# One streaming-encoder step: the input norm's gain row comes by DMA, and the first two x tiles are scaled before they are split

## The chip, the cores and the metric

The kernel runs on one core of a Trainium2 chip. The metric is device time in microseconds (us) of one execution, as a median of several. One execution was also taken by the hardware profiler, and every line of a profile below comes from such an execution.

The core has five engines that run their own instruction streams and wait for each other by semaphores: PE (matrix products and transposes), DVE (vector work), ACT (activations and copies), POOL (vector work as well) and SP, which here only issues transfers. PSUM is the memory that PE writes its products to; SBUF is the large on-chip memory.

## The reference

One layer on 2048 prompt frames and 64 frames of a running stream, width 1024, all in 32-bit floats:

```python
def rms_norm(x, g):
    xf = x.astype(jnp.float32)
    y = xf * lax.rsqrt(jnp.mean(xf * xf, axis=-1, keepdims=True) + EPS)
    return (y * g.astype(jnp.float32)).astype(x.dtype)

def mixer_layer(x, ln_g, w_in, lb, norm_g, w_out, attn_fn, s0):
    B, T, _ = x.shape
    aq, ak, av, ag, hq, hf, hi, hg = jnp.split(rms_norm(x, ln_g) @ w_in, SPLITS, axis=-1)
    heads = lambda a: a.reshape(B, T, H_A, DH_A)
    k = heads(ak)
    v = heads(av)
    o_a = attn_fn(heads(aq), k, v).reshape(B, T, W_A) * jax.nn.silu(ag)
    o_b, S = hgrn2_branch(hq, hf, hi, hg, lb, norm_g, s0)
    y = x + jnp.concatenate([o_a, o_b], axis=-1) @ w_out
    return y, k, v, S
```

`attn_fn` is a banded attention over 64-frame chunks (8 heads of 64), `hgrn2_branch` a gated linear recurrence whose forget gate is `f = lb + (1-lb) sigmoid(W_f x)` (4 heads of 128), with `lb` a softmax over two rows of `lb_gamma`. The result goes through a last RMSNorm. The change touches only how the first `rms_norm` and the first columns of `w_in` are brought to PE.

## The kernel before, in words

The frames are worked in four blocks of 512 to 576. For each block the normalised x is brought to PE as two parts that PE takes in its faster 32-bit form: `xh`, the rounded value, and `xl`, what rounding left. Each 128 columns of `w_in` (32 such pieces, "weights" below) are split in the same way into a pair `w[:, 0]` and `w[:, 1]`. `project` makes one piece of the projection by 8 products of xh by the first part, 8 of xl by the first part, and 8 of xh by the second part, added up in one PSUM tile `acc`. In the first block, the first two weights are used in two halves of 256 frames (x tiles 0 and 1, then x tiles 2 and 3), all others on 512 frames at once.

Before the first product the following must happen to each x tile of 128 frames (`x_tile`, `x_split`): it lands (SP's transfer), ACT squares and sums it (L368) and makes the reciprocal root (L336, L337), DVE scales it by that and by the gain row `ln_in_g` in two halves of 512 columns (L382), PE transposes four blocks of 128 columns at a time into a PSUM tile named tr, pv or g (L253), ACT rounds it to xh (L408), DVE subtracts to get xl (L412). Tile 3 and weights 2 and 3 land in the rooms `kd` and `v`, which the attention uses later, so the trace calls them so.

DVE's gain row must stand in all 128 partitions. Before, 4 KB of it are loaded into one partition, and two products of a row of ones by it (L1970) spread it over a PSUM tile `s`; DVE reads it there, and ACT copies it to SBUF later (L1948) for the other blocks. While nothing else is ready, PE runs products of the identity (`spinning`, L1959).

POOL rounds the first three weights (L462) and DVE the rest (L465); POOL makes all the second parts in four pieces of 256 columns (L470). Then the pair is stored to DRAM for the later blocks (L479). `forget_bounds` makes `lb` and `1 - lb` (`oml`) with four tiny DVE instructions (L302 to L305), which the first forget gate needs (L1249, L1250, then a running sum, L1256).

The order of the instructions on every engine is set by a planner (`Plan`), run when the program is built: threads of work say when they may go on, by times that it estimates for the engines or by conditions on what was issued, and the first ready thread of the best priority issues its next piece. Nothing is decided on the chip: each engine takes its list in order, and an instruction that waits holds all behind it on that engine. The planner's own clock only sets that order.

Of the kernel before, what the change touches and what calls it, by code (L numbers as in the profile page):

```python
# [17 lines left out]
P = 128  # L18
# [165 lines left out]
def hymba_step(  # L184
# [105 lines left out]
    def forget_bounds():  # L290

        lmx = T(cst, [P, NHB], F32, "lmx")
        le = T(cst, [P, 2, NHB], F32, "le")
        dve.tensor_tensor(lmx, lbg[:, 0], lbg[:, 1], ALU.max)
        for i in range(2):
            dve.tensor_sub(le[:, i], lbg[:, i], lmx)
        t = C.dve(300)
        yield lambda: "r1" in have
        act.activation(le, le, AF.Exp)
        t = C.act(8, t)  # L300
        yield lambda: "s1" in have
        dve.tensor_add(lmx, le[:, 0], le[:, 1])  # L302
        dve.reciprocal(lmx, lmx)
        dve.tensor_mul(lb, le[:, 0], lmx)
        dve.tensor_scalar(oml, lb, -1.0, 1.0, ALU.mult, ALU.add)  # L305
        C.dve(400, t)
        have.add("bounds")
# [43 lines left out]
    def x_tile(sb, half, c, here=None, gain=None):  # L351
# [21 lines left out]
        if not sb:  # L373
            yield lambda: "gain" in have and (not half or x_there.get((0, 0, 1), (0, 0))[0] == 4)
        g = g_in[:rows] if gain is None else gain
# [27 lines left out]
    def x_split(sb, half, c, rows, k0, tag, pt, t):  # L403
# [6 lines left out]
        there(sb, half, k0, 0, t)  # L410
        yield "D", t
# [23 lines left out]
    def weights():  # L435


        for j, (sb, nt) in enumerate(order):
            if sb:
                yield lambda: j - 1 in w_at  # L440
                yield from tk["w"].get()
                w = w_pair()
                sp.dma_start(f32(w), wd[nt])
                t = C.dma(1024)
                w_at[j] = (w, t, t)
                continue
# [9 lines left out]
    def w_split(j, nt, raw, t, tok):  # L456
# [4 lines left out]
        if j < 3:  # L461
# [7 lines left out]
        for k in range(0, KT, 2):  # L469
            pool.tensor_sub(w[:, 1, k : k + 2], raw[:, k : k + 2], f32(w[:, 0, k : k + 2]))  # L470
            t = C.pool(320, t)
            if k == 0:
                w_at[j] = (w, th, t + 2500.0)
            if k < KT - 2:
                yield "P", t - 300.0
# [59 lines left out]
    def project(j, ranges, evac, close=True, ready=None):  # L535
# [5 lines left out]
        for off, bn in ranges:  # L541
# [3 lines left out]
            for i, (wi, x) in enumerate(((0, xh), (0, xl), (1, xh))):  # L545
                if i == 2:
                    yield tl
                for kt in range(KT):
                    if ready and i < 2 and kt % 4 == 0:
                        yield lambda: ready(i, kt)  # L550
# [1357 lines left out]
    def program():  # L1908


        constants()
        kroom = f32(T(pa, [P, 2, WIN + NMAX], F32R, "kd")).rearrange("p a c -> p (a c)")
        vroom = f32(T(pa, [P, 2, 9, 2, 64], F32R, "v")).rearrange("p h t s d -> p (h t s d)")
        act.dma_start(g_in[0:1], ln_in_g.rearrange("(o d) -> o d", o=1))
# [10 lines left out]
        for what, i in (("x", 0), ("x", 1), ("w", 0), ("x", 2), ("w", 1), ("x", 3), ("w", 2), ("w", 3)):  # L1925
            if what == "x":
                sp.dma_start(xr0[i], x_rows(0, i * P, P))
            else:
# [6 lines left out]
        gps = s_ps()  # L1935
        tk["g"].take()
        tk["s_ps"].take()
# [3 lines left out]
        def first_x():  # L1941
            for c in range(4):
                C.spawn(x_tile(0, c // 2, c * P, (xr0[c], landed["x", c]),
                               gps.rearrange("p a c -> p (a c)")), 0)
            yield lambda: x_there.get((0, 1, 1), (0, 0))[0] == 4
            tk["xn"].put(3, C.now)
            yield "A", C.now
            act.copy(g_in, gps.rearrange("p a c -> p (a c)"))  # L1948
            tk["s_ps"].put(1, C.act(1024))
            for a in (f32(ql[64:128, 0]), f32(ql[0:64, 1])):  # L1950
                yield "P", 0.0
                pool.memset(a, 0.0)
                C.pool(300)
# [10 lines left out]
        for _ in range(4):  # L1964
            spinning()
            C.now += 400.0
            yield None

        for a in range(2):
            pe.matmul(gps[:, a], f32(ones)[0:1], g_in[0:1, a * 512 : a * 512 + 512], start=True, stop=True)  # L1970
            C.now += 1000.0
            yield None
        have.add("gain")
        for _ in range(3):
            spinning()
            C.now += 330.0
# [188 lines left out]
```

## Time and profile before

| what | us |
|---|---|
| median of three runs (1252.43 to 1253.24) | 1253.23 |
| the profiled execution, its own time | 1252.94 |
| its span, first to last instruction | 1251.2 |
| PE busy in it | 1237.5 (99%) |
| DVE, ACT, POOL busy | 888.8, 684.5, 412.4 |
| first product of the projection starts | 12.18 |
| PE runs on without a shown gap from | 23.78 |

The span is 1.7 us shorter than the execution's own time. In the rows of the timeline the columns are: start, duration, engine, line, operation, the tile written and the tiles read with their shape, how many alike were merged (the duration is then that of all), and in brackets the idle time before it and what ended it. PE's matmul records overlap, since its products are pipelined; the time from one to the next is what counts. Where the same row is said to have a pitch, that is this time.

### The profile page before, as it was taken

Reading aid. Unit: us, or ns where it says so; the run is one execution under the profiler, and the core shown is the slowest. Engines: PE = TensorE matmul, PEld = TensorE weight load, DVE = VectorE, ACT = ScalarE, POOL = GpSimd, SP = SyncE. Lnnn points to the kernel's source line nnn. Section 1 sums busy time; section 2 is a strip of 40 time slices with the busy share of each in tenths; the row PEclk is TensorE's granted clock in tenths of the full one; section 3 lists DMA queues with packets and bytes.
Section 4 is the critical chain, followed back from the end, with each engine's and each line's share of the span. In section 5 each row is a group of like instructions: output and inputs, shape, how many; then the busy total and the mean of one; then the engine's idle time right before and its main releaser. Section 6 shows DMA issues by size and latency. Waiting matters only on the chain. (4 is left out here: it accounts for less than half of the span.)

```text
span 1251.2 us, 21385 instructions
## 1 busy us (share of the span) xinstructions
PE 1237.5 (99%) x7526; PEld 1089.1 (87%) x7526; DVE 888.8 (71%) x1889; ACT 684.5 (55%) x1533; POOL 412.4 (33%) x702
## 2 busy tenths in 40 slices
PE   8999999999999999999999999999999999999997
PEld 7888888999999999998888888988888888888786
DVE  6688879766767677686576667775857476867775
ACT  6354546655556556674465556664656445643443
POOL 6766565111110110201233242133241103474543
PEclk9999999999999999999999999999999999999999
DMA  8987979666554476654777778677666665888431
GB/s 331 335 289 242 333 268 350 207 181 223 166 186 155 146 250 192 202 165 164 274 257 249 279 261 281 224 252 255 217 245 208 215 215 207 330 272 248 144 119 67
DMA packets 137956, 287.94 MB, mean 230 GB/s; under 512 B 35257, under 2 KB 79289, under 8 KB 120186
## 3 DMA queue, kind: packets, MB, share of 16 engines
q1 hardware_dynamic: 137560, 286.58, 67.7%
q8 instruction: 59, 0.97, 0.3%
q14 instruction: 47, 0.39, 0.1%
q10 hardware_dynamic: 290, 0.01, 0.0%
HBM read 195.31 MB, written 92.27 MB: 230 GB/s over the span
## 5 line engine op out<-in xcount | busy, mean ns | idle before, releaser
L249 PE MATMUL acc<-xh,w 128*128 128x512 f32 (+2 forms) x2752 | 568.7, 345 | 0.6 <-ACT xh L408 0.6
L249 PEld LDWEIGHTS acc<-xh,w 128*128 128x128 f32 x2752 | 437.7, 189 | 49.7 <-ACT xh L408 1.0
L249 PE MATMUL acc<-xl,w 128*128 128x512 f32 (+2 forms) x1376 | 292.8, 345 | 1.6 <-DVE xl L412 1.6
L249 PEld LDWEIGHTS acc<-xl,w 128*128 128x128 f32 x1376 | 220.8, 189 | 26.6 <-DVE xl L412 2.0
L946 ACT CAST ph<-tr 128x512 fp32r<-128x512 f32 (+3 forms) x176 | 87.9, 507 | 86.9 <-PE pv L249 48.9
L934 ACT ACTIVATE pr<-pr,nm 128x640 f32<-128x640 f32 (+4 forms) x132 | 100.6, 762 | 57.1 <-DVE nm L917 56.5
L470 POOL TENSOR_TENSOR w<-wraw,w 128x256 fp32r<-128x256 f32 x120 | 103.0, 886 | 55.1 <-DVE w L465 48.2
L917 DVE CUSTOM_DVE_ANT_0 pr<-s,bias 128x640 f32<-128x640 f32 (+4 forms) x128 | 94.4, 737 | 37.0 <-PE s L249 36.4
L949 DVE TENSOR_TENSOR ph<-tr,ph 128x512 fp32r<-128x512 f32 (+3 forms) x176 | 101.2, 589 | 25.9 <-ACT ph L946 25.1
L249 PE MATMUL pv<-ph,v 128*128 128x256 f32 (+2 forms) x344 | 97.7, 370 | 0.0
L253 PE MATMUL tr<-ident,pr 128*128 128x128 f32 x580 | 88.4, 272 | 0.9 <-DVE ph L949 0.5
L506 POOL TENSOR_TENSOR xn<-wraw,xn 128x256 fp32r<-128x256 f32 x48 | 39.5, 824 | 141.9 <-ACT xn L503 136.1
L988 DVE TENSOR_TENSOR mixa<-mixa,pv 64x256 f32<-64x256 f32 (+1 forms) x144 | 56.9, 395 | 35.5 <-ACT mixa L984 32.1
L1090 POOL TENSOR_TENSOR mixa<-mixa,sga 128x256 f32<-128x256 f32 (+1 forms) x36 | 28.5, 793 | 162.4 <-DVE mixa L988 150.5
L938 DVE TENSOR_SCALAR pr<-pr,sm 128x640 f32<-128x640 f32 (+4 forms) x132 | 76.3, 578 | 4.7
L253 PEld LDWEIGHTS tr<-ident,pr 128*128 128x128 f32 x580 | 69.8, 140 | 10.6 <-PE acc L249 0.8
L1527 POOL TENSOR_TENSOR k<-ob 128x512 f32<-128x512 f32 (+2 forms) x20 | 17.9, 893 | 179.9 <-ACT ob L1518 139.8
L570 ACT ACTIVATE sig<-acc 128x512 f32<-128x512 f32 (+2 forms) x64 | 32.1, 501 | 62.7 <-PE acc L249 59.9
L249 PEld LDWEIGHTS pv<-ph,v 128*128 128x128 f32 (+1 forms) x344 | 58.3, 189 | 7.0
L984 ACT COPY mixa<-pv 64x256 f32<-64x256 f32 (+1 forms) x72 | 25.2, 351 | 58.6 <-PE pv L249 54.3
L249 PE MATMUL s<-kd,q 128*128 128x320 f32 (+2 forms) x232 | 55.9, 311 | 0.4 <-DVE nm L917 0.4
L249 PE MATMUL s<-kd,ql 128*128 128x320 f32 (+2 forms) x232 | 55.5, 309 | 0.0
(324 smaller groups left out, 2134.5 us busy)
## 6 DMA issues: line engine op xcount, KB each, us to landing
w<-wd SPq DMA_DIRECT2D x96, 1024.0 KB, 5.5
wd<-w SPq DMA_DIRECT2D x32, 1024.0 KB, 7.6
wraw<-in_w_in_dram SPq DMA_DIRECT2D x30, 512.0 KB, 5.5
wod<-xn SPq DMA_DIRECT2D x28, 512.0 KB, 5.8
xn<-in_x_prompt_dram SPq DMA_DIRECT2D x23, 512.0 KB, 4.7
bias<-biasd SPq DMA_DIRECT2D x24, 320.0 KB, 5.4
carry<-kd SPq DMA_DIRECT2D x12, 512.0 KB, 7.0
carry<-v SPq DMA_DIRECT2D x12, 512.0 KB, 5.8
```

Source lines behind the costliest of these rows:

```text
L249: pe.matmul(out, w, x, **kw)
L253: pe.transpose(out, x, idn)
L470: pool.tensor_sub(w[:, 1, k : k + 2], raw[:, k : k + 2], f32(w[:, 0, k : k + 2]))
L506: pool.tensor_sub(f32r(st[:, c.start + 512 : c.stop + 512]), src[:, c], st[:, c])
L570: act.activation(sig[:, :bn], acc, AF.Exp, scale=-1.0)
L917: dve.tensor_tensor_reduce(s[:, :nk].rearrange("p (a c) -> p a c", a=ns), sps[:, :ns, :kn], d.bias[:, h, bcol : bcol + nk].rearrange("p (a ...
L934: act.activation(s[:, :nk], s[:, :nk], AF.Exp, bias=nm[:, 0:1], scale=-1.0, accum_out=sm)
L938: dve.tensor_scalar(s[:, :nk], s[:, :nk], sm, None, ALU.mult)
L946: act.copy(ph[:krows, 0, :wid], pt[:krows, :wid])
L949: dve.tensor_sub(ph[:krows, 1, :wid], pt[:krows, :wid], f32(ph[:krows, 0, :wid]))
L988: dve.tensor_add(mix[hs, :qn], mix[hs, :qn], pv[hs, i, :qn])
L1090: pool.tensor_mul(mix[:, :n], mix[:, :n], d.sg[:, g0 : g0 + n])
```

## The change

The gain row is loaded into all 128 partitions by one transfer on SP's queue, second in line, behind x tile 0. The two products, the PSUM tile for them, ACT's copy and the 4 KB transfer on ACT's queue go away, and DVE reads the gain in SBUF. x tiles 0 and 1 are scaled before either is split, and 2 and 3 likewise: a split's subtraction now waits (in the planner) until the second tile of its pair was scaled. The four instructions of `forget_bounds` wait for x tile 3's scaling where they waited for tile 1's. POOL rounds four weights and no longer three, and takes the pieces of a split without spacing. The two memsets of `ql` are issued at the start. `project` waits (again in the planner) for each quarter of a weight's second part, no longer for all of it. PE runs 12 products of the identity in place of 4, 2 products of ones and 3 more.

```diff
--- before.py
+++ after.py
@@ -298,7 +298,7 @@
         yield lambda: "r1" in have
         act.activation(le, le, AF.Exp)
         t = C.act(8, t)
-        yield lambda: "s1" in have
+        yield lambda: "s3" in have
         dve.tensor_add(lmx, le[:, 0], le[:, 1])
         dve.reciprocal(lmx, lmx)
         dve.tensor_mul(lb, le[:, 0], lmx)
@@ -348,7 +348,7 @@
     x_there = {}
     x_left = {(-1, 0): True, (-1, 1): True}
 
-    def x_tile(sb, half, c, here=None, gain=None):
+    def x_tile(sb, half, c, here=None):
 
         off, bn = SUPER[sb][3][half]
         rows = min(P, off + bn - c)
@@ -371,8 +371,8 @@
         t = C.act(1700, t)
         have.add(f"r{c // P}")
         if not sb:
-            yield lambda: "gain" in have and (not half or x_there.get((0, 0, 1), (0, 0))[0] == 4)
-        g = g_in[:rows] if gain is None else gain
+            yield lambda: not half or x_there.get((0, 0, 1), (0, 0))[0] == 4
+        g = g_in[:rows]
         cut = (slice(0, 512), slice(512, D)) if not sb else (slice(0, D),)
         ends = []
         for k0 in (0, 4):
@@ -408,6 +408,8 @@
         act.copy(dh, src)
         t = C.act(512, t)
         there(sb, half, k0, 0, t)
+        if not sb:
+            yield lambda: f"s{2 * half + 1}" in have
         yield "D", t
         dve.tensor_sub(dl, src, f32(dh))
         t = C.dve(512, t)
@@ -442,7 +444,7 @@
                 w = w_pair()
                 sp.dma_start(f32(w), wd[nt])
                 t = C.dma(1024)
-                w_at[j] = (w, t, t)
+                w_at[j] = (w, t, [t] * 4)
                 continue
             if j in raws:
                 raw, t, tok = raws.pop(j)
@@ -458,7 +460,7 @@
         yield lambda: j == 0 or j - 1 in w_at
         yield from tk["w"].get()
         w = w_pair()
-        if j < 3:
+        if j < 4:
             pool.tensor_copy(w[:, 0], raw)
             t = C.pool(700, t)
         else:
@@ -470,9 +472,10 @@
             pool.tensor_sub(w[:, 1, k : k + 2], raw[:, k : k + 2], f32(w[:, 0, k : k + 2]))
             t = C.pool(320, t)
             if k == 0:
-                w_at[j] = (w, th, t + 2500.0)
+                w_at[j] = (w, th, [])
+            w_at[j][2].append(t + 400.0)
             if k < KT - 2:
-                yield "P", t - 300.0
+                yield "P", 0.0
         if tok:
             tk[tok].put()
         yield t
@@ -543,9 +546,10 @@
             acc = acc_ps()
             n = 0
             for i, (wi, x) in enumerate(((0, xh), (0, xl), (1, xh))):
-                if i == 2:
-                    yield tl
                 for kt in range(KT):
+                    if i == 2 and kt % 2 == 0:
+                        yield lambda: len(tl) > kt // 2
+                        yield tl[kt // 2]
                     if ready and i < 2 and kt % 4 == 0:
                         yield lambda: ready(i, kt)
                     mm(acc[:, :bn], w[:, wi, kt, :], x[:, kt, off : off + bn], bn,
@@ -1909,9 +1913,10 @@
 
 
         constants()
+        for a in (f32(ql[64:128, 0]), f32(ql[0:64, 1])):
+            pool.memset(a, 0.0)
         kroom = f32(T(pa, [P, 2, WIN + NMAX], F32R, "kd")).rearrange("p a c -> p (a c)")
         vroom = f32(T(pa, [P, 2, 9, 2, 64], F32R, "v")).rearrange("p h t s d -> p (h t s d)")
-        act.dma_start(g_in[0:1], ln_in_g.rearrange("(o d) -> o d", o=1))
         act.dma_start(lbg, lb_gamma)
         act.dma_start(g_norm, hg_norm_g)
         xr0 = [T(px, [P, D], F32, "xn", bufs=XNB) for _ in range(3)] + [kroom[:, :D]]
@@ -1922,9 +1927,11 @@
                 tk[tag].take()
         landed = {}
         C.now = 900.0
-        for what, i in (("x", 0), ("x", 1), ("w", 0), ("x", 2), ("w", 1), ("x", 3), ("w", 2), ("w", 3)):
+        for what, i in (("x", 0), ("g", 0), ("x", 1), ("w", 0), ("x", 2), ("w", 1), ("x", 3), ("w", 2), ("w", 3)):
             if what == "x":
                 sp.dma_start(xr0[i], x_rows(0, i * P, P))
+            elif what == "g":
+                sp.dma_start(g_in, ln_in_g.rearrange("(o d) -> o d", o=1).broadcast_to([P, D]))
             else:
                 sp.dma_start(wr0[i], w_in[order[i][1]].rearrange("p (k n) -> p k n", k=KT))
             landed[what, i] = C.dma(640) - 1800.0
@@ -1932,25 +1939,15 @@
         for i in range(4):
             raws[i] = (wr0[i], landed["w", i], "raw" if i < 2 else None)
         spin = psum("g")
-        gps = s_ps()
         tk["g"].take()
-        tk["s_ps"].take()
         C.now = 1400.0
         C._on("P", 4000.0, 0.0)
 
         def first_x():
             for c in range(4):
-                C.spawn(x_tile(0, c // 2, c * P, (xr0[c], landed["x", c]),
-                               gps.rearrange("p a c -> p (a c)")), 0)
+                C.spawn(x_tile(0, c // 2, c * P, (xr0[c], landed["x", c])), 0)
             yield lambda: x_there.get((0, 1, 1), (0, 0))[0] == 4
             tk["xn"].put(3, C.now)
-            yield "A", C.now
-            act.copy(g_in, gps.rearrange("p a c -> p (a c)"))
-            tk["s_ps"].put(1, C.act(1024))
-            for a in (f32(ql[64:128, 0]), f32(ql[0:64, 1])):
-                yield "P", 0.0
-                pool.memset(a, 0.0)
-                C.pool(300)
             yield lambda: 3 in w_at
             tk["kv0"].put()
             tk["kv1"].put()
@@ -1961,19 +1958,9 @@
         C.spawn(first_x(), 0)
         C.spawn(forget_bounds(), 1)
         C.spawn(weights(), 2)
-        for _ in range(4):
+        for _ in range(12):
             spinning()
-            C.now += 400.0
-            yield None
-
-        for a in range(2):
-            pe.matmul(gps[:, a], f32(ones)[0:1], g_in[0:1, a * 512 : a * 512 + 512], start=True, stop=True)
-            C.now += 1000.0
-            yield None
-        have.add("gain")
-        for _ in range(3):
-            spinning()
-            C.now += 330.0
+            C.now += 440.0
             yield None
         tk["g"].put()
 
```

The planner then puts the instructions in another order. At three places:

DVE, the first two x tiles and the step to the next two, before. x tiles 0 to 3 are xn_171, xn_172, xn_173 and kd_166; lmx, lb and oml belong to the forget gate's bounds; tr, pv and g are PSUM tiles with transposes; s_186 is the gain in PSUM:

```order
L382 SCALAR_TENSOR_TENSOR xn_171<-xn_171,rstd_201,s_186 128x512 x2
L382 SCALAR_TENSOR_TENSOR xn_172<-xn_172,rstd_210,s_186 128x512
L412 TENSOR_TENSOR xl_154<-tr_215,xh_153 128x4x128
L382 SCALAR_TENSOR_TENSOR xn_172<-xn_172,rstd_210,s_186 128x512
L302 TENSOR_TENSOR lmx_188<-le_189 128x4
L303 RECIPROCAL lmx_188<-lmx_188 128x4
L304 TENSOR_TENSOR lb_81<-le_189,lmx_188 128x4
L305 TENSOR_SCALAR oml_82<-lb_81 128x4
L412 TENSOR_TENSOR xl_154<-tr_225,xh_153 128x4x128
L412 TENSOR_TENSOR xl_154<-pv_231,xh_153 128x4x128
L412 TENSOR_TENSOR xl_154<-tr_246,xh_153 128x4x128
L382 SCALAR_TENSOR_TENSOR xn_173<-xn_173,rstd_262,s_186 128x512 x2
```

The same place with the change (x tiles 0 to 3 are xn_172, xn_173, xn_174 and kd_168, and gin_152 is the gain in SBUF):

```order
L382 SCALAR_TENSOR_TENSOR xn_172<-xn_172,rstd_203,gin_152 128x512 x2
L382 SCALAR_TENSOR_TENSOR xn_173<-xn_173,rstd_221,gin_152 128x512 x2
L414 TENSOR_TENSOR xl_154<-tr_212,xh_153 128x4x128
L414 TENSOR_TENSOR xl_154<-tr_225,xh_153 128x4x128
L414 TENSOR_TENSOR xl_154<-pv_235,xh_153 128x4x128
L414 TENSOR_TENSOR xl_154<-g_246,xh_153 128x4x128
L382 SCALAR_TENSOR_TENSOR xn_174<-xn_174,rstd_262,gin_152 128x512 x2
L382 SCALAR_TENSOR_TENSOR kd_168<-kd_168,rstd_285,gin_152 128x512 x2
L414 TENSOR_TENSOR xl_154<-tr_297,xh_153 128x4x128
```

All four halves of tiles 0 and 1 are scaled first, the four subtractions follow without a break, the bounds have gone from here, and then tiles 2 and 3 are scaled together.

DVE, from there to the last subtraction of tiles 2 and 3, before (w_346 is weight 3, sig and gk are the forget gate, gb its running sum, gq another gate):

```order
L382 SCALAR_TENSOR_TENSOR kd_166<-kd_166,rstd_277,s_186 128x512
L412 TENSOR_TENSOR xl_154<-tr_300,xh_153 128x4x128
L382 SCALAR_TENSOR_TENSOR kd_166<-kd_166,rstd_277,s_186 128x512
L1249 TENSOR_SCALAR sig_318<-sig_318,oml_82,lb_81 128x256
L1250 TENSOR_SCALAR gk_310<-sig_318 128x256
L465 CAST w_346<-v_167 128x1024
L412 TENSOR_TENSOR xl_154<-tr_325,xh_153 128x4x128
L412 TENSOR_TENSOR xl_154<-pv_333,xh_153 128x4x128
L1256 SCALAR_TENSOR_TENSOR gb_311<-reset_78,sig_318 128x256
L412 TENSOR_TENSOR xl_154<-tr_355,xh_153 128x4x128
L575 TENSOR_TENSOR gq_309<-acc_312,sig_382 128x256
```

And with the change:

```order
L414 TENSOR_TENSOR xl_154<-tr_297,xh_153 128x4x128
L302 TENSOR_TENSOR lmx_189<-le_190 128x4
L303 RECIPROCAL lmx_189<-lmx_189 128x4
L304 TENSOR_TENSOR lb_81<-le_190,lmx_189 128x4
L305 TENSOR_SCALAR oml_82<-lb_81 128x4
L414 TENSOR_TENSOR xl_154<-tr_316,xh_153 128x4x128
L1253 TENSOR_SCALAR sig_339<-sig_339,oml_82,lb_81 128x256
L1254 TENSOR_SCALAR gk_337<-sig_339 128x256
L414 TENSOR_TENSOR xl_154<-pv_324,xh_153 128x4x128
L414 TENSOR_TENSOR xl_154<-g_355,xh_153 128x4x128
L579 TENSOR_TENSOR gq_336<-acc_307,sig_381 128x256
L1260 SCALAR_TENSOR_TENSOR gb_338<-reset_78,sig_339 128x256
```

The bounds now stand between the subtractions of tile 2's two halves, behind all the scaling; the rounding of weight 3 has left DVE; the running sum has moved behind the last subtraction.

POOL, the first weights, before (w_221, w_265, w_296 and w_346 are the pairs of weights 0 to 3):

```order
L462 CAST w_221<-wraw_174 128x1024
L470 TENSOR_TENSOR w_221<-wraw_174,w_221 128x256 x3
L462 CAST w_265<-wraw_175 128x1024
L470 TENSOR_TENSOR w_221<-wraw_174,w_221 128x256
L470 TENSOR_TENSOR w_265<-wraw_175,w_265 128x256
L462 CAST w_296<-kd_166 128x1024
L470 TENSOR_TENSOR w_265<-wraw_175,w_265 128x256 x2
L470 TENSOR_TENSOR w_296<-kd_166,w_296 128x256
L470 TENSOR_TENSOR w_265<-wraw_175,w_265 128x256
L470 TENSOR_TENSOR w_296<-kd_166,w_296 128x256
L470 TENSOR_TENSOR w_346<-v_167,w_346 128x256
L470 TENSOR_TENSOR w_296<-kd_166,w_296 128x256
```

And with the change, where these are w_233, w_275, w_361 and w_391, and w_464 and w_473 are weights 4 and 5:

```order
L1917 MEMSET ql_155 64x704 x2
L464 CAST w_233<-wraw_175 128x1024
L472 TENSOR_TENSOR w_233<-wraw_175,w_233 128x256 x4
L464 CAST w_275<-wraw_176 128x1024
L472 TENSOR_TENSOR w_275<-wraw_176,w_275 128x256 x4
L464 CAST w_361<-kd_168 128x1024
L472 TENSOR_TENSOR w_361<-kd_168,w_361 128x256
L464 CAST w_391<-v_169 128x1024
L472 TENSOR_TENSOR w_361<-kd_168,w_361 128x256 x3
L472 TENSOR_TENSOR w_391<-v_169,w_391 128x256 x4
L472 TENSOR_TENSOR w_464<-wraw_266,w_464 128x256 x4
L472 TENSOR_TENSOR w_473<-wraw_344,w_473 128x256 x4
```

Weights 0 and 1 are now done one after the other, weight 3 is rounded here, and the memsets of ql stand ahead of all. On SP the list is x0, gain, x1, w0, x2, w1, x3, w2, w3 where it was the same without the gain. From a little over half of the program on, all five engines have the same instructions in the same order as before.

## The prediction, made before the changed kernel was run

> **What bounds the kernel now.** I read the page first, then PE's list of waits, then the timelines of PE, DVE, POOL and ACT over the first 35 us, the only part that the change is written for.
>
> ```profile
> span 1251.2 us, 21385 instructions
> PE 1237.5 (99%) x7526; PEld 1089.1 (87%) x7526; DVE 888.8 (71%) x1889; ACT 684.5 (55%) x1533; POOL 412.4 (33%) x702
> ```
>
> PE has work in 99% of the span, so only what PE loses can be won: 13.7 us in all. Its longest wait:
>
> ```profile
> PE acc L249 <- DVE xl L412: 1.6, 2, 1.4
> ```
>
> It lies at the start. On PE:
>
> ```profile
> 7.14 1.65 PE L1959 MATMUL g<-ident 128*128 128x128 f32 x6
> 8.58 1.91 PE L253 MATMUL tr<-ident,xn 128*128 128x128 f32 x8
> ...
> 12.18 0.72 PE L249 MATMUL acc<-xh,w 128*128 128x256 f32 x4
> ...
> 15.23 1.34 PE L249 MATMUL acc<-xl,w 128*128 128x256 f32 x8 [1.39 <-DVE xl L412]
> ...
> 17.13 0.60 PE L253 MATMUL tr<-ident,xn 128*128 128x128 f32 x4
> ...
> 20.94 2.16 PE L249 MATMUL acc<-xh,w 128*128 128x256 f32 x16
> 22.94 0.64 PE L249 MATMUL acc<-xl,w 128*128 128x256 f32 x4
> 23.78 0.74 PE L249 MATMUL acc<-xl,w 128*128 128x256 f32 x4 [0.20 <-DVE xl L412]
> ...
> 31.84 3.79 PE L249 MATMUL acc<-xh,w 128*128 128x512 f32 x16
> ```
>
> Products begin at 12.18, stop until the xl of tiles 0 and 1 is there at 15.23, and run on from then but for a short stop at 23.78, which waits for the last xl of tiles 2 and 3. From 23.78 PE is fed. **So the change is worth what it does to that moment, 23.78: the last xl of tile 3**, and DVE makes it. An earlier 15.23 counts only if the lead lives until there.
>
> **Step 1, transfers.** ACT's rows:
>
> ```profile
> 4.64 1.06 ACT L368 ACTIVATE ck<-xn 128x1024 bf16<-128x1024 f32 x1 [2.55 <-DMA xn<-in_x_prompt_dram]
> ...
> 6.32 1.04 ACT L368 ACTIVATE ck<-xn 128x1024 bf16<-128x1024 f32 x1
> ...
> 7.82 0.20 ACT L337 ACTIVATE rstd<-rstd 128x1 f32<-128x1 f32 x1
> ...
> 12.46 0.59 ACT L408 CAST xh<-tr 128x512 fp32r<-128x512 f32 x1 [0.71 <-PE tr L253]
> ...
> 14.45 0.20 ACT L337 ACTIVATE rstd<-rstd 128x1 f32<-128x1 f32 x1
> ...
> 16.05 0.20 ACT L337 ACTIVATE rstd<-rstd 128x1 f32<-128x1 f32 x1
> ```
>
> POOL's first row, and the stretch 6 to 8 us of the view by windows (last two columns: DMA share and GB/s):
>
> ```profile
> 7.39 1.04 POOL L462 CAST w<-wraw 128x1024 fp32r<-128x1024 f32 x1 [4.04 <-DMA wraw<-in_w_in_dram]
> ...
> 6.00:8.00 2.00, 2.00 (x6) 0.86 (x5) 1.07 (x5) 1.90 (x7) 0.61 (x1) 1.00 1.04 408
> ```
>
> The DMA engines are full (share 1.04, 408 GB/s), so the 512 KB of the gain push all behind it back by 0.524 MB/408 GB/s = 1.29 us (x1 and w0 take (7.39-4.64)/2 = 1.37 each). Bounds: nothing, if one re-read row came for free, and two such transfers, 2.6. I take 1.29, nearest to both rows: x0 4.64, gain 5.93, x1 7.22, w0 8.68, w1 and the rest 1.29 later too.
>
> **Step 2, tiles 0 and 1.** Before, DVE waited for the gain's product:
>
> ```profile
> 7.33 2.07 DVE L382 SCALAR_TENSOR_TENSOR xn<-xn,rstd,s 128x512 f32<-128x512 f32 x3 [0.75 <-issue]
> ...
> 10.91 0.74 DVE L382 SCALAR_TENSOR_TENSOR xn<-xn,rstd,s 128x512 f32<-128x512 f32 x1
> 11.56 0.74 DVE L302 TENSOR_TENSOR lmx<-le 128x4 f32<-128x4 f32 x1
> ...
> 13.90 0.68 DVE L412 TENSOR_TENSOR xl<-tr,xh 128x512 fp32r<-128x512 f32 x1
> ...
> 15.10 0.68 DVE L412 TENSOR_TENSOR xl<-tr,xh 128x512 fp32r<-128x512 f32 x1
> ```
>
> Tile 0 gains: its root is there at about 6.4 (1.7 behind 4.64, see tile 1), so two scalings at a pitch of 0.66 (2.07 for three) end by 7.75. Tile 1 decides. Its squares start at 7.22, its root takes 1.70 as before (6.32 to 8.02), so 8.92. Now DVE reads both operands in SBUF while POOL works there, and the trace shows what that does:
>
> ```profile
> 8.52 2.10 POOL L470 TENSOR_TENSOR w<-wraw,w 128x256 fp32r<-128x256 f32 x3
> ...
> 30.77 5.39 POOL L470 TENSOR_TENSOR w<-wraw,w 128x256 fp32r<-128x256 f32 x5 [0.63 <-DVE w L465]
> ...
> 30.95 1.11 DVE L1346 TENSOR_TENSOR bm<-gb 128x512 f32<-128x512 f32 x1
> 31.99 1.23 DVE L1352 TENSOR_TENSOR bl<-gb 128x512 f32<-128x512 f32 x1
> ...
> L1855 DVE SCALAR_TENSOR_TENSOR pr<-pr,rstd,gin x6: 739/746/1078, 1139.2 to 1247.3; 128x512 f32<-128x512 f32 x6
> ```
>
> POOL's pieces, 0.69 apart alone (2.10 for three), are 1.15 apart beside DVE's SBUF instructions, and these 1.04 to 1.15: the two take turns. The four tiny instructions of the bounds, 128x4 each, lasted 2.34 us (11.56 to 13.90) beside POOL's work, and scalings from PSUM beside the same work kept their 0.74. The scaling by gin in SBUF has the middle 0.746 and the longest 1.08: a turn lost or not. So tile 1 pays between nothing and a POOL instruction a half, and I take turns, since POOL is never out of work here. POOL's rounding of w0 holds 8.68 to 9.69; tile 1 is scaled at 9.69 and, behind one POOL piece, at 11.05, done at 11.70 (before, 11.65). Its last xh is therefore cast at about 12.46 as before, and products start no earlier. The four subtractions, 0.60 apart (three of them from 13.90 to 15.10) and without the bounds among them, end at 14.1, not 15.78: xl products start at 13.6, not 15.23. **A lead of 1.6 us.**
>
> [...]
>
> **Step 3, tiles 2 and 3.** ACT squares them behind tile 1's last cast, which didn't move, so the roots stay at 14.65 and 16.25. POOL has done weight 0 at about 13.7 and rounds weight 1 until 14.75; then scalings and pieces take turns, 1.35 a pair (0.66+0.69): 14.8, 16.15, 17.5, 18.85, done at 19.5. Before:
>
> ```profile
> 15.70 1.40 DVE L382 SCALAR_TENSOR_TENSOR xn<-xn,rstd,s 128x512 f32<-128x512 f32 x2
> 17.01 0.74 DVE L382 SCALAR_TENSOR_TENSOR kd<-kd,rstd,s 128x512 f32<-128x512 f32 x1
> 18.99 0.74 DVE L382 SCALAR_TENSOR_TENSOR kd<-kd,rstd,s 128x512 f32<-128x512 f32 x1
> 19.73 0.41 DVE L1249 TENSOR_SCALAR sig<-sig,oml,lb 128x256 f32<-128x256 f32 x1
> 20.18 0.29 DVE L1250 TENSOR_SCALAR gk<-sig 128x256 f32<-128x256 f32 x1
> ...
> 23.07 0.66 DVE L412 TENSOR_TENSOR xl<-tr,xh 128x512 fp32r<-128x512 f32 x1
> ...
> 26.93 0.75 DVE L1249 TENSOR_SCALAR sig<-sig,oml,lb 128x256 f32<-128x256 f32 x1 [0.21 <-ACT sig L1246]
> 27.72 0.71 DVE L1250 TENSOR_SCALAR gk<-sig 128x256 f32<-128x256 f32 x1
> ```
>
> PE's transposes of tile 3 wait for these, with tile 0's and 1's products queued behind them; the xh products that stood at 21.9 (the second eight of the row at 20.94) come at about 21.1, and the lead is 0.8.
>
> **Step 4, the tail of DVE's list.** Between the last scaling and the last subtraction DVE now does: a subtraction 0.60, the bounds 2.34, a subtraction 0.60, the forget gate's two instructions 1.50, two subtractions 0.60 and 0.66: 6.3 us, so 19.5 to 25.8. Before it was 19.7 to 23.73. The bounds have come in here; and the gate's two, which ran at 19.73 in 0.66 with POOL idle (it had nothing to do until DVE had rounded weight 3), now meet a POOL that rounds weights 2 and 3 itself, as at 26.93, where they took 1.50 (to 28.43). If POOL lets them pass, bounds 0.5 and gate 0.66: 23.1. If the first also waits out a rounding: 1.04 more, 26.8. I take the rows that had POOL busy.
>
> **The sum.** PE goes on with the last four xl products at 25.86, not 23.78: +2.1 us; ends 23.2 and 26.9 give -0.6 and +3.1. Removed besides: ACT's copy of 1.0 (ACT idles 45%), PE's two products (other identity products stand there): nothing. POOL's extra rounding, 1.04, and its lost turns are covered: weight 2's second part is made by 27 and read from about 34 on (the second eight of PE's row at 31.84). The new quarter waits cost nothing, as each quarter lies ahead of its use by 0.7 or more. Profiled execution 1252.94 + 2.1 = 1255.0; its median lies 0.29 over it, so **1255.3**, and with some of the turns won, I say 1255.2.
>
> **Rivals.** (a) *Turns are rarely lost.* Then tile 1 is scaled by 10.3, tile 3 by 17.6, and the last xl of tile 3 waits for PE and ACT alone, about 22.0: -1.8 us, 1251.4. For it: 0.746 as the middle for gin; against it: in the late rows POOL is mostly elsewhere. (b) *POOL becomes the bound.* Each turn that DVE wins delays weight 1's second part, which is ready at 20.05 with its last quarter read at 20.8; if the transfer of the gain takes the upper bound, or the bounds wait out a rounding, that slack of 0.75 is gone and PE waits for POOL, then for DVE at 26.9: +3.1 to +4.5, about 1256.9. It decides from 0.75 us of delay on. (c) *Slow PE clock.* The first transposes are 0.21 apart (8 in 1.91), those at 17.13 0.11 (4 in 0.60), so PE speeds up only after steady work. Twelve identity products, two records each, end at 6.7, and transposes alone follow with gaps; 24 products at twice the pitch of 0.12 would cost 2.9, but of this all but some 0.5 lies in the wait for DVE: 1255.7. [...] (d) *The rest of the order.* The first half's pieces are mixed anew. PE's waits from 24 to 1000 us are, but for xl's,
>
> ```profile
> PE s L249 <- DVE nm L917: 0.4, 1, 0.4
> PE acc L249 <- ACT xh L408: 0.4, 1, 0.4
> ```
>
> so 0.8 can be won there or as much lost.
>
> **Numbers.** Forecast 0.47; (a) 0.23, (b) 0.18, (c) 0.07, (d) alone 0.05. About 0.2% (2.5 us) is what a measurement can tell here: faster is below 1250.7, slower above 1255.7. Slower: (b) 0.15, half of (c) 0.04, a quarter of the forecast 0.12: 0.31. Faster: a quarter of (a) with (d): 0.06. Same: 0.63. Range 1251.0 to 1257.5; the forecast's own is 1253.0 to 1256.4.
>
> **What would show it.** Right: scalings by gin from 9 us on last 1.0 to 1.4; xl products first at 13.6; bounds of 2 us behind 19 us; PE's longest wait 2 to 3 us on xl near 22 to 26. Wrong: scalings of 0.75, that wait gone, or PE waiting for POOL's second part or for the gain's landing.

## The result and the profile after

| | before | after |
|---|---|---|
| median, us (lowest to highest) | 1253.23 (1251.68 to 1254.31) | 1256.48 (1254.93 to 1257.82) |
| the profiled execution, us | 1252.94 | 1256.39 |
| its span, us | 1251.2 | 1254.7 |

The ratio is 1.0027 with a 95% interval of 1.0017 to 1.0037: the change costs 3.25 us, 0.27%. Forecast was 1255.2, in a range of 1251.0 to 1257.5, with "within 0.2%" as the likeliest class; it came out just beyond that bound, which lies inside the interval.

PE's list of waits of the changed kernel (us in total, times, longest):

```profile
PE pv L253 <- DVE xn L382: 2.2, 1, 2.2
PE acc L249 <- DVE xl L414: 2.1, 1, 2.1
PE tr L253 <- DVE xn L382: 1.8, 1, 1.8
```

All three lie in the first 26 us. PE's and DVE's rows of the timeline there:

```profile
13.17 2.10 PE L249 MATMUL acc<-xh,w 128*128 128x256 f32 x8
...
15.11 1.12 PE L249 MATMUL acc<-xl,w 128*128 128x256 f32 x8
...
25.05 1.97 PE L249 MATMUL acc<-xl,w 128*128 128x256 f32 x8 [2.13 <-DVE xl L414]
...
26.82 2.87 PE L249 MATMUL acc<-xh,w 128*128 128x256 f32 x16
...
33.28 1.07 PE L249 MATMUL acc<-xl,w 128*128 128x512 f32 x4
```

```profile
6.89 1.42 DVE L382 SCALAR_TENSOR_TENSOR xn<-xn,rstd,gin 128x512 f32<-128x512 f32 x2 [1.25 <-ACT rstd L337]
9.93 2.35 DVE L382 SCALAR_TENSOR_TENSOR xn<-xn,rstd,gin 128x512 f32<-128x512 f32 x2 [1.63 <-ACT rstd L337]
...
14.17 0.69 DVE L414 TENSOR_TENSOR xl<-g,xh 128x512 fp32r<-128x512 f32 x1
15.79 1.96 DVE L382 SCALAR_TENSOR_TENSOR xn<-xn,rstd,gin 128x512 f32<-128x512 f32 x2 [0.92 <-ACT rstd L337]
17.67 2.36 DVE L382 SCALAR_TENSOR_TENSOR kd<-kd,rstd,gin 128x512 f32<-128x512 f32 x2
...
19.95 0.68 DVE L414 TENSOR_TENSOR xl<-tr,xh 128x512 fp32r<-128x512 f32 x1
...
20.55 0.40 DVE L302 TENSOR_TENSOR lmx<-le 128x4 f32<-128x4 f32 x1
...
22.67 0.68 DVE L414 TENSOR_TENSOR xl<-tr,xh 128x512 fp32r<-128x512 f32 x1
...
23.27 0.40 DVE L1253 TENSOR_SCALAR sig<-sig,oml,lb 128x256 f32<-128x256 f32 x1
...
24.92 0.67 DVE L414 TENSOR_TENSOR xl<-g,xh 128x512 fp32r<-128x512 f32 x1
```

Beside a working POOL a pair of scalings takes 1.96 to 2.36 us where it took 1.40 from PSUM. The first pair, at 6.89, reads the same gain in SBUF and takes 1.42: POOL is idle then, its first rounding starts at 9.57. So it is not the place of the gain alone that costs, but the place together with POOL's work. The bounds take 20.55 to 22.67; the last xl is there at 24.92 + 0.67 = 25.59. Before it was 23.73: **1.86 us later**.

But the program is later than that. A good mark is the first product of 512 columns by xl, since the same work lies ahead of it in both kernels. It starts at 33.28; before:

```profile
30.03 1.98 PE L249 MATMUL acc<-xl,w 128*128 128x512 f32 x8
```

That is 3.25 us, and the span ends 3.5 us later, so all but some 0.2 of the loss is made ahead of this mark. The other 1.39 is seen in the view by windows of the changed kernel (PE, PEld, DVE, ACT, POOL busy, then the granted clock, the DMA share, GB/s):

```profile
11.00:13.00 2.00, 1.40 (x7) 1.04 (x8) 2.00 (x4) 0.59 (x1) 2.00 (x3) 0.64 1.03 418
13.00:15.00 2.00, 2.00 (x11) 1.89 (x10) 1.77 (x3) 1.45 (x3) 2.00 (x3) 0.51 1.01 401
15.00:17.00 2.00, 2.00 (x18) 2.00 (x18) 1.22 (x2) 1.90 (x7) 1.92 (x3) 1.00 1.03 219
...
25.00:26.00 1.00, 0.95 (x5) 0.95 (x6) 1.00 (x3) 0.00 (x0) 1.00 (x2) 0.60 1.04 430
26.00:27.00 1.00, 1.00 (x6) 1.00 (x6) 0.91 (x1) 0.00 (x0) 1.00 (x2) 0.50 0.94 393
27.00:28.00 1.00, 1.00 (x7) 1.00 (x6) 0.00 (x0) 0.00 (x0) 1.00 (x2) 0.50 0.99 410
28.00:29.00 1.00, 1.00 (x8) 1.00 (x8) 0.00 (x0) 0.24 (x1) 0.12 (x1) 0.69 0.73 303
```

The granted clock is half in two stretches. The first stretch, about 11.6 to 15.0, has the eight xh products of 13.17 start 15.11 - 13.17 = 1.94 us ahead of what follows, 0.24 each, where the eight of 15.11 start 0.12 apart. The second follows the 2.13 us in which PE waited for xl. Adding up 1 - clock and doubling, it is slow for 3.4 us ((0.40+0.50+0.50+0.31)/0.5). In the kernel before, the view has 1.00 in all windows from 4 to 32 us. For the first of them that cannot be right, since the transposes at 8.58 stand 0.21 apart (8 in 1.91) and those at 17.13 0.11; from the transposes at 11.79 (4 in 0.63) on the products agree with it.

### The profile page after: what moved, and what is told of

Same layout as the page of the kernel before. It is cut to its first block, busy times and chain, and to the rows that moved or that the text cites. A ratio compares the mean times of both kernels' runs of the same rounds, so it can differ in the third digit from the quotient of the medians.

```text
span 1254.7 us, 21384 instructions
## 1 busy us (share of the span) xinstructions
PE 1236.8 (99%) x7532; PEld 1090.8 (87%) x7532; DVE 891.9 (71%) x1888; ACT 683.5 (54%) x1532; POOL 415.7 (33%) x703
```

## The experiments

Two numbers are read from every trace: when the last xl of tile 3 is there, and when the first 512-wide xl product starts. Both stand as differences to the kernel before (23.73 and 30.03), with the stop of PE in front of those xl products. These and the span are of the one profiled execution of each kernel, which can lie off its kernel's median: H's and A's took 1.2 and 0.9 us more than theirs, E's 0.9 less.

| kernel | last xl | stop of PE | 512-wide product | span | median ratio, 95% |
|---|---|---|---|---|---|
| the change | +1.86 | 2.13 | +3.25 | +3.5 | 1.0027 (1.0017 to 1.0037) |
| A, only the gain by DMA | +3.52 | 0.80 | +3.53 | +5.1 | 1.0030 (1.0017 to 1.0042) |
| B, only the new order | -0.91 | 1.47 | -0.91 | +1.55 | 1.0014 (1.0005 to 1.0023) |
| C, order and DMA, gain in PSUM | -0.55 | 0.75 | -0.55 | +0.6 | 1.0004 (0.9994 to 1.0013) |
| D, bounds early | +1.53 | 0.56 | +1.54 | +1.95 | 1.0022 (1.0013 to 1.0032) |
| E, POOL rounds three | +2.08 | 1.49 | +2.14 | +3.5 | 1.0036 (1.0024 to 1.0047) |
| F, PE filled, in g | +2.01 | 2.05 | +6.04 | +7.4 | 1.0055 (1.0040 to 1.0070) |
| F2, PE filled, in s | +1.96 | 0.35 | +1.96 | +2.3 | 1.0024 (1.0014 to 1.0034) |
| H, B with bounds in the middle | -1.85 | none | -1.70 | +1.7 | 1.0005 (0.9996 to 1.0014) |
| G, before, DVE regrouped | -1.96 | none | -1.54 | -1.3 | 0.9993 (0.9984 to 1.0002) |
| I, G with bounds in POOL's pause | -2.22 | 0.13 | -2.21 | -1.4 | 0.9985 (0.9976 to 0.9994) |

Where PE waits for that xl, the two columns agree within 0.06 us, but for the change itself (1.39 more, the slow clock) and F. So the prediction's pivot, DVE's last xl, is the right one.

### A and B: each half of the change alone

A is the kernel before with the gain by DMA and DVE reading it in SBUF, in the old order (with 12 identity products at the start, as in the change). B is the change with the gain spread by the two products into PSUM, as before.

```diff
 A, in before.py:
-        yield lambda: "gain" in have and (not half or ...)
+        yield lambda: not half or ...
-  x_tile(0, c // 2, c * P, (xr0[c], landed["x", c]), gps...)
+  x_tile(0, c // 2, c * P, (xr0[c], landed["x", c]))
+  elif what == "g":
+      sp.dma_start(g_in, ln_in_g....broadcast_to([P, D]))
 B, in after.py:
-  for what, i in (("x", 0), ("g", 0), ("x", 1), ...
+  for what, i in (("x", 0), ("x", 1), ...
+  pe.matmul(gps[:, a], f32(ones)[0:1], g_in[0:1, ...])
+  x_tile(0, c // 2, c * P, (xr0[c], landed["x", c]), gps...)
```

> The kernel before with one part of the change alone: the gain row comes by the 512 KB transfer and DVE reads it in SBUF (and PE runs 12 identity products at the start, as in the change); the order of scalings, subtractions and bounds, POOL's three roundings and the waits for a whole weight stay as they were. Theory (turns of DVE and POOL, then a slow PE): the transfer and the turns hurt here as well, 1255 to 1257 us. Rival (the new order, with the bounds late and POOL rounding four weights, is what costs): 1253 to 1254 us.

> The changed kernel with the gain as it was before: 4 KB by ACT's queue, two products into PSUM, DVE reads it there; order, bounds, POOL's four roundings and quarter waits as changed. Theory: scalings of 0.74 again, tile 3 scaled by about 17, the last xl of tile 3 by 23, so 1252 to 1253.5 us. Rival (order): 1255 us or more.

A lost 3.5 us by the mark, B won 0.9: the loss comes with the gain by DMA, and the new order wins at the start. DVE and PE in A:

```profile
16.86 2.31 DVE L382 SCALAR_TENSOR_TENSOR xn<-xn,rstd,gin 128x512 f32<-128x512 f32 x2
...
21.25 0.69 DVE L412 TENSOR_TENSOR xl<-tr,xh 128x512 fp32r<-128x512 f32 x1 [0.94 <-ACT xh L408]
...
26.58 0.67 DVE L412 TENSOR_TENSOR xl<-tr,xh 128x512 fp32r<-128x512 f32 x1
```

```profile
16.39 2.08 PE L249 MATMUL acc<-xl,w 128*128 128x256 f32 x8 [0.40 <-DVE xl L412]
...
19.54 1.05 PE L253 MATMUL tr<-ident,xn 128*128 128x128 f32 x4
```

The slow scalings come with the gain in SBUF, in the old order as well. But they are not all of A's loss. A's mean granted clock over the whole run is 0.995, where the kernel before has 0.999, and its PE runs at half pace here: the 14 products ahead of tile 2's transposes take 3.15 us, 16.39 to 19.54, 0.22 apart, where at 0.12 they would take 1.7; the xh cast from these transposes is what DVE waits for, 0.94 us at 21.25. Up to 0.9 of A's 3.5 us is thus the clock's, by this estimate. What had not been expected: B's lead is gone at the end (-0.91 became +1.55). H, below, shows where.

### C: the transfer kept, the operand back in PSUM

C moves the 512 KB as the change does, but nobody waits for it at the start; DVE reads the gain in PSUM, made from a row of its own. A against B still mixes transfer and operand; C tells them apart.

```diff
+        grow = [T(wk, [P, 512], F32, "sig", bufs=2) for _ in range(2)]
+            pe.matmul(gps[:, a], f32(ones)[0:1], grow[a][0:1], ...)
+                C.spawn(x_tile(..., gps.rearrange("p a c -> p (a c)")), 0)
```

> As the one with the order only, but the 512 KB transfer of the gain row stands in SP's queue where the change has it (DVE still scales from PSUM). Theory of turns: scalings of 0.74, tile 1 done by 11.3 and not 12.2, tile 3 by 18.7 and not 20.0, PE's stop on xl shrinks from 2.1 to about 1, total 1253.7 to 1254.8 us. Rival (the 2.1 us by which the transfer makes everything behind it late is the whole cost): no gain beyond 0.3 us, 1256 to 1256.5 us.

DVE in C:

```profile
9.99 1.41 DVE L382 SCALAR_TENSOR_TENSOR xn<-xn,rstd,s 128x512 f32<-128x512 f32 x2 [1.25 <-ACT rstd L337]
...
15.02 1.41 DVE L382 SCALAR_TENSOR_TENSOR xn<-xn,rstd,s 128x512 f32<-128x512 f32 x2 [0.92 <-ACT rstd L337]
16.62 1.41 DVE L382 SCALAR_TENSOR_TENSOR kd<-kd,rstd,s 128x512 f32<-128x512 f32 x2 [0.20 <-ACT rstd L337]
...
18.55 0.15 DVE L302 TENSOR_TENSOR lmx<-le 128x4 f32<-128x4 f32 x1
...
20.22 0.68 DVE L414 TENSOR_TENSOR xl<-tr,xh 128x512 fp32r<-128x512 f32 x1
...
22.50 0.68 DVE L414 TENSOR_TENSOR xl<-g,xh 128x512 fp32r<-128x512 f32 x1
```

Every pair takes 1.41. From C to the change the mark moves by 3.25 + 0.55 = 3.80 us: 2.41 of it is the last xl (25.59 for 23.18) and 1.39 the clock. The 2.41 is 0.77 at the start of tile 2's scaling (15.79 for 15.02), 1.23 in tile 2's and 3's scalings (from there to 19.95 for 17.95), and 0.45 in the bounds (19.95 to 22.67 for 17.95 to 20.22). From B to C, the transfer, it is only 0.36.

The transfer does arrive late. The GB/s over the first 14 us in 40 equal slices of 0.35 us, of the change:

```profile
GB/s 0 0 0 0 0 152 164 283 307 318 319 329 247 223 211 212 200 283 422 398 445 386 433 421 421 410 410 410 445 421 410 410 445 410 398 421 421 410 410 386
```

And of the kernel before:

```profile
GB/s 0 0 0 0 0 47 199 269 339 386 445 375 400 413 357 412 399 364 388 398 421 445 375 421 410 468 386 421 410 421 421 433 375 421 410 410 234 202 196 193
```

From 4.2 to 6.0 us (the 13th to the 17th slice), just ahead of the gain's first use near 6.9, only 200 to 247 GB/s move, where 357 to 413 moved before. Tile 1's squares start at 8.19 (6.32 before) and POOL's first rounding at 9.57 (7.39 before): 1.9 and 2.2 us later, not the 1.29 of 512 KB at full rate. (Before, tile 1's squares stood behind tile 0's root on ACT, so 2.2 is nearer to what the landing moved.) At tile 2's scaling C is still 0.91 us behind B, 15.02 for 14.11. That only 0.36 is left at the last xl is luck: the forget gate's two instructions take 1.07 us in C (20.82 to 21.89) and 1.67 in B (19.87 to 21.54).

### D: the bounds early

```diff
 in after.py, forget_bounds:
-        yield lambda: "s3" in have
+        yield lambda: "s1" in have
```

> The changed kernel with the bounds' condition as before (tile 1 scaled), which puts the four instructions back among tile 1's subtractions. Theory (2.1 us of bounds in front of the last xl): PE's stop on the last xl shrinks by 1 to 1.5 us, its stop on the first xl grows by as much as it can spare; 1254.5 to 1255.7 us. Rival (the bounds' place doesn't matter, only turns of the scalings do): 1256.2 us or more.

DVE in D:

```profile
12.78 0.15 DVE L302 TENSOR_TENSOR lmx<-le 128x4 f32<-128x4 f32 x1
...
14.17 0.68 DVE L414 TENSOR_TENSOR xl<-tr,xh 128x512 fp32r<-128x512 f32 x1
...
15.96 2.44 DVE L382 SCALAR_TENSOR_TENSOR xn<-xn,rstd,gin 128x512 f32<-128x512 f32 x2
18.32 2.67 DVE L382 SCALAR_TENSOR_TENSOR kd<-kd,rstd,gin 128x512 f32<-128x512 f32 x2
...
24.59 0.67 DVE L414 TENSOR_TENSOR xl<-g,xh 128x512 fp32r<-128x512 f32 x1
```

Taking 2.1 us of bounds out of the tail wins 0.33 us of the last xl: the scalings start no earlier and lose more turns (15.96 to 20.92 for the four, 4.96 us; 15.79 to 19.95 in the change, 4.16). PE's stop is 0.56, and no slow clock follows (the eight xl products at 24.73 take 1.17). The bounds' place is worth little as long as DVE is slowed in the scalings; what D won, 1.7 us at the mark, is mostly the clock. In its median the gain is 0.9 us against the change, with overlapping intervals.

### E: POOL's fourth rounding

```diff
-        if j < 4:
+        if j < 3:
             pool.tensor_copy(w[:, 0], raw)
```

> The changed kernel with weight 3 rounded by DVE again (behind the last xl), POOL rounding three. Theory: the forget gate's two instructions and the bounds meet one POOL rounding less, 0.3 to 1 us off the last xl, 1255.3 to 1256.1 us. Rival (POOL's fourth rounding is what makes DVE late): back to 1254 us or less.

The last xl is there no earlier (25.81): in this execution tile 1's x landed later (squares at 8.69 for 8.19), and from tile 2's first scaling to the last xl DVE takes 9.53 us for 9.80, 0.27 less, just under the 0.3 to 1 expected. PE never waits for POOL in either, and the median is no better: the rival that POOL is the bound falls. E's mark is 1.1 us better than the change's for another reason. Its stop of PE is shorter:

```profile
25.26 1.34 PE L249 MATMUL acc<-xl,w 128*128 128x256 f32 x8 [1.49 <-DVE xl L414]
26.43 2.15 PE L249 MATMUL acc<-xh,w 128*128 128x256 f32 x16
```

Eight products take 1.17 us, not 1.77: the clock stayed at full (1.00 from 24 to 30 us). E then loses 1.3 us behind the mark.

### F and F2: work for PE in its wait

Identity products are put between the second half's xh and xl products, to keep PE busy in its wait. F put nine of them into a bank of the tile g, F2 eight into the free bank s. They add work whose result nobody reads.

```diff
 in project (F2; F has psum("g")):
+                if i == 1 and not j and off:
+                    yield from tk["s_ps"].get()
+                    fill = s_ps()
+                    for _ in range(8):
+                        pe.matmul(fill[:, 0, :P], ident, ident, start=True, stop=True)
+                    tk["s_ps"].put(1, C.now)
```

> The changed kernel with 9 more identity products on PE between the xh and the xl products of the first weight's second half, where PE waits 2.1 us for DVE; they take 2.0 us at the fast pitch. Theory (PE slows down in that wait and then runs 24 products at 0.21 in place of 0.12): those products run at 0.12, 1.6 us won, about 1254.8 us. Rival (the slow products have another cause, or PE's wait is all that counts): 1256.3 us or slightly more.

> The changed kernel with 8 more identity products between the xh and the xl products of the first weight's second half, in a PSUM bank that nothing else uses yet, so that they can run while PE waits for DVE (1.8 us of the 2.3 from 22.8 on). Theory (the wait lets PE's clock fall, and 24 products at 0.21 in place of 0.12 cost 1.6 us after it): those products run at 0.12; the 512-wide xl products start 1.6 us earlier than in the changed kernel, 31.7, and the total is about 1254.9 us. Rival (the clock falls whatever stands in the wait, or the time comes back later): 33.3 and 1256.3 us or more.

F was badly built: that bank of g was still to be read by DVE's last subtraction, so the filling itself waited for it and then stood ahead of the products, and the clock fell as well (below). In F:

```profile
25.79 2.90 PE L553 MATMUL g<-ident 128*128 128x128 f32 x18 [2.05 <-DVE xl L414]
28.34 2.05 PE L249 MATMUL acc<-xl,w 128*128 128x256 f32 x8
```

In F2 it ran in the wait:

```profile
22.85 1.95 PE L553 MATMUL s<-ident 128*128 128x128 f32 x16
25.15 1.33 PE L249 MATMUL acc<-xl,w 128*128 128x256 f32 x8 [0.35 <-DVE xl L414]
...
31.99 1.98 PE L249 MATMUL acc<-xl,w 128*128 128x512 f32 x8
```

From the first xl product to the mark it is 31.99 - 25.15 = 6.84 us, and 33.28 - 25.05 = 8.23 in the change: 1.39 us, with DVE as late as in the change. F2's granted clock is 1.00 from 24 to 30 us. So the slow clock is caused by PE's stop, and it is the rest of the loss. The medians (1255.97 and 1256.48) agree with that in sign but cannot tell 0.5 us.

### H: where B's lead goes

H is B with the bounds behind tile 1's last subtraction. It was to have the whole lead and no stop of PE.

```diff
 in B, forget_bounds:
-        yield lambda: "s3" in have
+        yield lambda: x_there.get((0, 0, 1), (0, 0))[0] == 4
```

> The version with the gain in PSUM and the new order (1254.8 us, 0.9 us ahead of the kernel before when the 512-wide xl products start), with the bounds between the last subtraction of tile 1 and the first scaling of tile 2, where DVE idles 0.8 us. Theory: the last xl of tile 3 comes about 1.4 us earlier and the first products of tile 2 0.8 later, so these products start at 28.4 to 28.9, 1.2 to 1.7 us ahead of before. If a lead at the start lasts, the total is 1251.3 to 1252 us; rival (what is won at the start is lost to the new order behind it, as in that version): 1253 to 1255 us.

At the mark it leads by 1.70, at the end it is 1.7 late. PE's waits in H:

```profile
PE tr L253 <- DVE ph L953: 1.3, 1, 1.3
...
PE pv L249 <- ACT eb L1359: 0.6, 1, 0.6
...
PE pv L249 <- DVE v L662: 0.3, 1, 0.3
```

The second and third lie at 88 and 82 us and do not exist in the kernel before, whose PE is busy from 80 to 90 us without a break. Product for product H's PE is 1.70 us ahead at the mark, about 0.1 at 100 us, 0.16 at 600 and 0.03 at 805, then 0.53 behind at 815 and 1.66 behind at 1090. So of the 3.4 us lost from the mark to the end some 1.6 goes before 100 us, 0.9 of it in these two stops, 0.6 near 810 us, and 1.1 net near 1085, where the wait of 1.3 was 0.46.

Only the first part can be laid to the lists themselves: from 566 us on PE's list is that of the kernel before, and so are those of the other engines from 536 to 562 us on. Near 1085 us it is a transfer that lands later. DVE's and PE's work there is queued behind this cast of ACT, which stood at 1080.43 before, after a wait of 1.26:

```profile
1082.09 0.62 ACT L1686 CAST xh<-sig 128x512 fp32r<-128x512 f32 x1 [2.38 <-DMA sig<-mixd]
```

It is not that an early PE meets a late transfer: H was late here already, G, as early at the mark, keeps its lead, and A, 4.4 us late at 1060 us, waits 1.67 at the same cast and loses 0.6 there. Why the transfer lands when it does is open. So is which of the change's edits (quarter waits, memsets, POOL's fourth rounding) makes the lists behind the mark worse by the 1.6 us.

### G and I: the grouping alone, in the old order

G is the kernel before with the lists of PE, ACT, POOL and SP as they are, and DVE's regrouped: tile 1's second scaling ahead of tile 0's first subtraction, the bounds behind tile 1's last subtraction, the running sum behind tile 3's last. I moves the bounds once more, to right ahead of the first forget gate, near 18 us, when POOL waits for DVE's rounding of weight 3.

```diff
 G:
+        held["tile 1 split"].append(four)
+            held["tile 1 scaled"].append(lambda: dve.tensor_sub(dl, src, f32(dh)))
+                held["tile 3 split"].append(scan)
 I, to G:
-        held["tile 1 split"].append(four)
+        held["gate"].append(four)
+            let("gate")
             dve.tensor_scalar(f[:, :bn], f[:, :bn], oml[:, h : h + 1], ...)
```

> The kernel before, with the orders of PE, ACT, POOL and SP left as they are; only DVE's list is regrouped at the start: tile 1's second scaling ahead of tile 0's first subtraction, the four instructions of the bounds behind tile 1's last subtraction instead of among them, and the running sum of L1256 behind the last subtraction of tile 3. The gain stays in PSUM, so no scaling takes turns with POOL. The theory that the lead of the change's grouping is real and is lost only to the SBUF operand: the last xl lands at 22.2 to 22.5 us (23.72 before), the first 512-wide xl product starts at 28.3 to 28.9 us (30.03 before); if the rest of the program keeps that lead, the total is 1251.3 to 1252.0 us. Rival: the later stretches are set by transfers, and a PE that comes 1.4 us early waits there that much longer (the wait near 1086 us grows from 0.46 us): 1252.5 to 1253.2 us, with the lead still seen at 100 us and gone at the end. Rival two: regrouping DVE alone gives no lead because POOL's roundings end last there: first 512-wide xl product at 29.7 to 30.1 us, total 1253.2.

> The regrouped kernel before (gain in PSUM, the two scalings of a pair together, the running sum behind the last subtraction) with one more move on DVE: the four instructions of the bounds stand right ahead of the first forget gate, behind tile 3's scaling, near 18 us, where POOL has nothing to do until DVE has rounded weight 3 (POOL idle 2.75 us there in the regrouped kernel). All other engines' lists are as before. Theory that DVE's tiny instructions are slow only while POOL works: the four take 0.4 to 0.7 us, not 1.96, so tile 2 is scaled from about 14.5 (its root) instead of 15.18 and the last xl is there at 20.6 to 21.2 (21.77 in the regrouped kernel, 23.73 before); PE's products then set the moment, first 512-wide xl product at 27.6 to 28.0 (28.49 and 30.03), total 1250.6 to 1251.6. Rival: they take about 2 us wherever they stand, so the last xl is at 21.8 or later and the product at 28.4 to 28.6, total 1252.1 as in the regrouped kernel. Second rival: PE earlier by another 0.7 us only waits for transfers later, total 1252 with the lead seen at 100 us but not at the end.

DVE in I:

```profile
17.49 0.16 DVE L310 TENSOR_TENSOR lmx<-le 128x4 f32<-128x4 f32 x1
...
18.37 0.41 DVE L1268 TENSOR_SCALAR sig<-sig,oml,lb 128x256 f32<-128x256 f32 x1
...
20.83 0.68 DVE L427 TENSOR_TENSOR xl<-tr,xh 128x512 fp32r<-128x512 f32 x1
```

POOL's rows there show why:

```profile
16.45 0.75 POOL L488 TENSOR_TENSOR w<-kd,w 128x256 fp32r<-128x256 f32 x1
19.79 0.74 POOL L488 TENSOR_TENSOR w<-v,w 128x256 fp32r<-128x256 f32 x1 [2.59 <-DVE w L483]
```

With POOL idle the four take 0.88 us, from 17.49 to 18.37; beside a working POOL they took 2.34 (before), 2.12 (the change), 1.96 (13.22 to 15.18 in G) and 1.39 (D). G starts the mark's product at 28.49 and ends 1.3 us earlier, but its interval (0.9984 to 1.0002) does not exclude no change. I starts it at 27.82 and ends 1.4 us earlier in its trace; its median is 1251.51 us against 1253.35, ratio 0.9985 (0.9976 to 0.9994): **1.8 us less than the kernel before**, with an interval wholly below 1, and so less than the changed kernel too. The mark and the total are as expected; the last xl, 21.51, is later than the 20.6 to 21.2 expected, since the four took 0.88 and not 0.4 to 0.7. It is only 0.26 ahead of G's; what moves the mark by 0.67 is that tile 2 is scaled from 13.97 and no longer from 15.18, behind the bounds, so that PE's transposes of it, after which PE never waits in G, come at 14.81 for 16.01. Of the 2.21 us at the mark 0.8 is gone at the end, as the second rival had it: 0.4 and 0.3 near 44 and 313 us, and 0.1 net near 1085 us, where PE waits 0.86 for 0.46 but a wait of 0.39 at 1073 us is gone. PE's list is the same in G, I and the kernel before; that the early arrival itself is what is given back is not shown.

## Why the prediction was right, and where not

- **The pivot** (the last xl of tile 3 sets what the change is worth) held for DVE's part: it sets the mark to 0.06 us in every kernel whose PE waited for it at full clock.
- **Step 1, the transfer.** Its size was wrong, about 2.2 us for 1.29, inside the bounds; its price at the last xl was 0.36 us (B to C), by luck, as 0.91 at tile 2's scaling shows. The reading of the full rate, 408 GB/s, was the error: while the gain comes, 200 to 247 GB/s move.
- **Step 2, tiles 0 and 1.** The turns were right: two scalings of tile 1 take 2.35, from 9.93, forecast 9.69 to 11.70. The lead of 1.6 us at the first xl product was not: 15.11 for 15.23, 0.12. The four subtractions ended at 14.86, not 14.1, and the products themselves ran at half clock from 13.17.
- **Step 3, tiles 2 and 3.** "The roots stay" failed: they came 1.1 us later (scaling at 15.79, not 14.8), as ACT's squares queue behind tile 1's cast, and this moved. The four scalings took 4.2 us, forecast 4.7, and ended at 20.03, not 19.5.
- **Step 4, the tail.** Forecast 6.3 us, measured 25.59 - 20.03 = 5.56: bounds 2.12 for 2.34, the gate's two 1.05 for 1.50. The errors of steps 3 and 4 cancel, +0.5 and -0.7: that 25.59 comes so near to 25.8 is in part luck.
- **The sum** had +2.1 and one cause. It is +1.86 for DVE and +1.39 for the clock: the missing term. Rival (c) had a slow PE at the start, seen at 11.6 to 15.0 us, and said that the wait for DVE hides all but 0.5 of it; the stop of 2.13 us ahead of the last xl products agrees for what PE's own products lost. It did not ask what the 2 us stop, which the sum itself forecast, does to the clock next. That term carried the result from "within 0.2%" to slower. That PE speeds up only after steady work was (c)'s estimate from two rows; no run tests it alone.
- **Rivals.** (a), turns rarely lost, falls with the scaling rows of A, D and the change. (b), POOL as the bound, falls with E. (d), the rest of the order, is 0.2 us in the change, but 2.5 to 3.4 in B and H, far above the 0.8 allowed; of H's 3.4, though, 1.7 goes where all lists are the same.

C against the change shows what the gain's place does: a pair takes 1.41 us with the gain in PSUM, 1.96 to 2.36 with it in SBUF beside POOL, and 1.42 with it in SBUF while POOL is idle. POOL pays as well: the four pieces of weight 0 and those of weight 1 take 3.57 and 4.16 us in the change (from 10.69 and 15.32), 2.81 and 2.82 in C (from 10.78 and 14.65). The bounds, 128x4 each, take 1.4 to 2.3 us beside POOL and 0.88 without it, as would follow if they take part in the same turns.

## What to carry to other kernels

Beside a busy POOL, an operand that DVE reads from PSUM was worth two products of PE here: moving it to SBUF cost 2.4 us on eight small instructions and what stands behind them. Put tiny DVE instructions where POOL pauses: four of them took 0.88 us there and 1.4 to 2.3 beside its work. Price a stop of PE not by its length alone: ask whether the clock falls behind it (1.39 us more behind a stop of 2.13 in the change, nothing behind 0.35 in F2), and fill it with products into a bank that nobody is still reading.

## What was not expected of the hardware

A stop of PE of 2.13 us halved the granted clock for 3.4 us in a stretch that is at full clock ahead of it and behind it, and 2.05 us in F did the same; stops of 1.47 and 1.49 us at the same place (B and E) did not. In the change the clock fell some 0.2 us after PE had restarted, in F some 1.5 us after it (0.63 is the mean of the window from 27 to 28 us, 1.00 before). Added up in the same way, the slow stretch that lies behind the first transposes is 3.4 us long in the change and 6.8 in E and in F2. In D and F the four transposes at 11.18 and 11.36 take 1.12 and 1.11 us, and the eight xh products behind them 2.25 in both, where 0.60 and 1.20 are the full pace; in A such rows reach from 11.09 (4 transposes in 1.12) to 19.54 (4 in 1.05).

The length of one stop does not decide it alone: in E the clock had already fallen at about 9.8 us (0.70 is the mean from 9 to 11), 0.2 us into a stop, with 1.3 us of transposes and a stop of 1.6 ahead of it. What else decides it these runs do not show.

While the gain's transfer, the same 4 KB read 128 times, was under way in the change, 200 to 247 GB/s moved, where 357 to 413 moved at that time in the kernel before.
